# The score scale put into the queries, the head biases loaded a head ahead from ScalarE's queue, and the first read-back products put on GpSimd

## The chip, the cores and the metric

The kernel runs on one core of one Trainium2 chip. The metric is the device time of one execution in microseconds. Three timed runs of the kernel before took 1576.5, 1576.89 and 1585.75 us; the median is 1576.89 us.

## What is computed

One encoder layer on a sequence of 1024 frames of width 1024, in float32. From a layer-normed, modulated input `h` one projection gives queries, keys and values of two attention branches of 8 heads each (head width 64) and two gates. The part of the reference that this change touches:

```python
# A) forgetting attention (FoX)
logits = einsum('bqhd,bkhd->bhqk', qb, k) * scale          # scale = 1/sqrt(64)
logits = logits + cq[:, :, :, None] - cum[:, :, None, :]   # cum = cumsum(log sigmoid(f))
logits = where(k_pos <= q_pos, logits, neg)
out = softmax(logits) @ v
# B) chunked attention, 64-frame chunks, own chunk and 8 to the left
logits = einsum('bcqhd,bckhd->bchqk', qc, kb) * scale
logits = logits + bias                                     # rel_table[h, clipped distance]
out = softmax(where(valid, logits, neg)) @ vb
# after both branches
merged = sigmoid(gate_a) * (o_a @ w_br_fox) + sigmoid(gate_c) * (o_c @ w_br_chunk)
mix = merged @ w_out
x = layer_norm(alpha * x + (1 + g1) * mix)
```

A second sub-layer follows (up-projection, causal depthwise convolution, SiLU gate, down-projection, layer norm).

## The kernel before

Every float32 product is made of three TensorE passes over operands split into a high part and a rest (`mm3`, lines 191 to 194). The layer runs in stages: modulation and the first transposes; attention (from about 100 to 720 us of the profile), in which the projections of later heads are worked off between the scores of earlier ones; the merge of the branches and the output projection; the up-projection; the down-projection.

**Attention.** The heads are worked through in pairs `ip`, in the order 4, 5, 6, 7 (chunked branch), 2, 3, 0, 1 (forgetting branch), and in each pair head by head. One head has four steps `g` of two blocks of 128 queries. The code is written so that, at step `n`, the scores of step `n + 1` stand ahead of the weighted sums of step `n`. `scores` (line 425) makes one block: two matmuls `pss` (L434, L435), then on VectorE one fused operation (L448) that adds the head's bias to the scores, scales, and keeps the row maximum `mx`, then the exponential on ScalarE (L454). `probs` turns the result by TensorE transposes `pst` (L488) and splits it on ScalarE (L491) and VectorE (L492) into `pt`; `weighted` multiplies it with the values (`pso`, L502).

**The bias of a head.** `prep` (line 384) is called for a head some steps before its first scores. It fills `m2`, a copy of the keys with its two halves of partitions exchanged (two DMAs, L392 and L393), and then loads the bias, all on SyncE's DMA queue: `fb`, one row of 1024 sums of the forget gate sent to all 128 partitions (L396), or `cb`, 128x640 numbers of the relative table (L399). There are two bias buffers. The raw scores are not scaled, so the bias has to be divided by the scale: `fb` is stored so (L334), and `cb` is multiplied in place by `scaled()` (line 405) on VectorE (L409), which then fills the two 64x64 corners outside the band with a large negative number (L410, L411). `scaled()` is called where the next step belongs to another head, ahead of the scores of that step.

**GpSimd.** Beside attention GpSimd prepares later weights (`side_work`): products and sums for the modulation, splits and differences, with its own loads and stores of 512 KB. The sums go through two buffers `acc` and are gathered on TensorE (`psada`, L163).

**Softmax sums.** Once per two pairs `inverted` (line 457) turns the sums of a pair, takes reciprocals into `rt` (L463), and stores them to `rd`. `rt` takes a buffer of the tag `fm`, of which there are two; in the forgetting branch the masked diagonal biases `fm` (L441) go through the same two.

**Reading back.** The unnormalised outputs of the heads are stored to `od` (`o32`). `load_o` (line 778) loads two pairs of half a sequence from `od` into `ost` and their reciprocals from `rd` into `ort`, multiplies them on VectorE (L786), and splits the product into `oh` and `ol` (L789, L790). Its first half is called for the pairs 4, 6, 2 and 0, three of them ahead of the last projections.

**The order of the work.** What is written is reordered when the program is built: the build places the instructions of each engine by its own estimate of when their operands are there, and keeps to that order. Each engine then works its own queue strictly in that order: an instruction that waits holds everything behind it on its engine. DMAs are issued by an instruction on the queue of SyncE, ScalarE or GpSimd, and the same holds for them.

## Time and profile before

| what | value |
|---|---|
| timed runs | 1576.5, 1576.89, 1585.75 us |
| profiled execution, its own time | 1572.65 us |
| its span from first to last instruction | 1570.9 us |
| TensorE busy | 1509.7 us, 96% |
| VectorE busy | 1081.9 us, 69% |
| ScalarE busy | 708.2 us, 45% |
| GpSimd busy | 641.5 us, 41% |
| granted TensorE clock, mean | 0.990 |

The time of the profiled execution is the span and 1.75 us around it. In the rows, PE is TensorE and PEld its loads of stationary operands, DVE is VectorE, ACT ScalarE, POOL GpSimd and SP SyncE; a `q` behind the engine marks its queue, as where a DMA is issued. `out<-in` are the program's names, without buffer numbers. A view of waits reads: engine, name and line that waited, after the arrow what ended the wait, then microseconds in total, how many times, and the longest. A view of stretches gives, for each stretch of the span, its length, the busy time of each engine with its instructions, the mean granted clock of TensorE, the busy share of the DMA engines and what they moved.

### The profile page before, as it was taken

The numbers are of one execution on the slowest core, as the hardware profiler recorded it, in microseconds if no ns is written. First come the engines' busy times: TensorE is split into PE (matmuls) and PEld (weight loads), VectorE is DVE, ScalarE is ACT, GpSimd is POOL, SyncE is SP. The second block draws the span as 40 slices with busy tenths as digits, with TensorE's granted clock in tenths as the row PEclk, the third lists the DMA queues.
The fourth block names the chain that finished last, engine by engine and source line by source line (L and its number), as shares of the span: only waits on it lengthen the run. The fifth ranks groups of instructions, "written<-read, shape, count | busy, mean of one in ns | idle before, by whom it ended". The sixth has DMA issues, their size and how long they took to land.

```text
span 1570.9 us, 21838 instructions
## 1 busy us (share of the span) xinstructions
PE 1509.7 (96%) x7663; PEld 1268.5 (81%) x7663; DVE 1081.9 (69%) x2161; ACT 708.2 (45%) x1316; POOL 641.5 (41%) x579
## 2 busy tenths in 40 slices
PE   6999989999999999899998999999999999999996
PEld 3788788889888888788886887888888888788885
DVE  6747566567757676564449488677778876845798
ACT  3545444554445454342102256445454454555451
POOL 0038988888788876100000003545445453000000
PEclk9999999999999999999999999999999999999999
DMA  9156665756666788426999676344333332697552
GB/s 370 40 168 221 216 207 198 233 194 201 220 202 201 253 280 273 172 99 228 307 339 336 242 255 207 104 173 155 133 121 120 129 112 103 223 342 256 196 187 76
DMA packets 130399, 317.81 MB, mean 202 GB/s; under 512 B 12897, under 2 KB 21809, under 8 KB 130289
## 3 DMA queue, kind: packets, MB, share of 16 engines
q1 hardware_dynamic: 94192, 207.79, 39.5%
q0 software_dynamic: 24432, 88.88, 16.6%
q10 hardware_dynamic: 11664, 19.75, 3.4%
q8 instruction: 60, 0.98, 0.3%
q14 instruction: 51, 0.41, 0.1%
HBM read 223.73 MB, written 84.25 MB: 196 GB/s over the span
## 4 chain that ended last, share of the span: by engine, by line
PE 80%; DVE 9%; DMA 7%; issue 2%; ACT 1%; SPq 0%; DVEq 0%; ACTq 0%
PE psu L852 24%; PE pso L502 4%; PE psd L1270 4%; PE psd L1271 4%; PE psd L1269 4%; PE pst L488 3%; PE psg L192 3%; PE psg L193 3%; PE psg L194 3%; PE psq L193 3%; PE psq L194 3%; PE psq L192 3%; DMA cb<-in_rel_t 2%; PE pss L434 2%; PE pss L435 2%; PE psv L295 2%
## 5 line engine op out<-in xcount | busy, mean ns | idle before, releaser
L852 PE MATMUL psu<-hc,wx 128*128 128x512 f32 x792 | 185.7, 389 | 0.1
L852 PEld LDWEIGHTS psu<-hc,wx 128*128 128x128 f32 x792 | 148.6, 188 | 31.4 <-ACT u L1195 0.5
L1118 DVE SCALAR_TENSOR_TENSOR pcv<-u,convp,pcv 128x1024 f32<-128x1024 f32 x88 | 113.2, 1286 | 45.4 <-ACT pcv L1116 44.5
L454 ACT ACTIVATE s<-s,mx 128x640 f32<-128x640 f32 (+7 forms) x128 | 94.5, 738 | 78.6 <-DVE mx L448 77.0
L1259 DVE TENSOR_TENSOR op<-rw,op 128x512 fp32r<-128x512 f32 x146 | 93.3, 688 | 52.9 <-ACT op L1258 52.6
L1258 ACT CAST op<-rw 128x512 fp32r<-128x512 f32 x146 | 85.2, 623 | 84.3 <-PE psd L1271 40.8
L1270 PE MATMUL psd<-op,op 128*128 128x512 f32 x292 | 113.6, 389 | 1.0 <-DVE op L1259 1.0
L1271 PE MATMUL psd<-op,op 128*128 128x512 f32 x292 | 113.6, 389 | 0.0
L491 ACT CAST pt<-pst 128x512 fp32r<-128x512 f32 (+1 forms) x192 | 82.5, 450 | 68.8 <-PE pst L488 67.3
L1269 PE MATMUL psd<-op,op 128*128 128x512 f32 x292 | 113.1, 389 | 0.0
L987 POOL DMA_DIRECT2D xd<-xr x8 | 4.3, 542 | 263.1 <-DVE xr L985 263.1
L192 PE MATMUL psq<-h1h,wh 128*128 128x512 f32 x256 | 104.4, 409 | 1.7 <-DVE h1h L188 1.3
L492 DVE TENSOR_TENSOR pt<-pst,pt 128x512 fp32r<-128x512 f32 (+1 forms) x192 | 96.5, 519 | 13.2 <-ACT pt L491 11.3
L192 PE MATMUL psg<-h1h,wh 128*128 128x512 f32 x256 | 104.6, 409 | 0.0
L194 PE MATMUL psg<-h1h,wl 128*128 128x512 f32 x256 | 100.6, 393 | 1.5 <-DVE wl L112 1.5
L194 PE MATMUL psq<-h1h,wl 128*128 128x512 f32 x256 | 101.2, 395 | 0.9 <-DVE wl L112 0.9
L193 PE MATMUL psq<-h1l,wh 128*128 128x512 f32 x256 | 101.5, 396 | 0.0
L193 PE MATMUL psg<-h1l,wh 128*128 128x512 f32 x256 | 100.7, 393 | 0.0
L502 PE MATMUL pso<-pt,vs 128*128 128x256 f32 x608 | 93.2, 292 | 6.4 <-DVE pt L492 6.2
L550 POOL TENSOR_SCALAR dr<-dr,cond 128x512 f32<-128x512 f32 x56 | 95.7, 1711 | 5.1 <-DMA dr<-in_w_ada 4.1
L502 PEld LDWEIGHTS pso<-pt,vs 128*128 128x128 f32 x608 | 82.9, 194 | 15.2 <-DVE pt L492 8.5
L488 PE MATMUL pst<-ident,s 128*128 128x128 f32 x528 | 83.7, 275 | 8.9 <-DVE pt L492 8.7
(284 smaller groups left out, 4013.7 us busy)
## 6 DMA issues: line engine op xcount, KB each, us to landing
ws<-in_w_up SPq DMA_DIRECT2D x34, 512.0 KB, 3.8
dr<-in_w_ada POOLq DMA_DIRECT2D x32, 512.0 KB, 4.7
dr<-in_w_down POOLq DMA_DIRECT2D x22, 512.0 KB, 5.2
td<-dr POOLq DMA_DIRECT2D x22, 512.0 KB, 5.4
rw<-td SPq DMA_DIRECT2D x44, 256.0 KB, 4.6
yd<-y SPq DMA_DIRECT2D x20, 512.0 KB, 2.8
rw<-yd SPq DMA_DIRECT2D x40, 256.0 KB, 4.6
rw<-sd SPq DMA_DIRECT2D x33, 256.0 KB, 4.6
```

Source lines behind the costliest of these rows:

```text
L192: pe.matmul(ps, wh, xh, start=start, stop=False)
L193: pe.matmul(ps, wh, xl, start=False, stop=False)
L194: pe.matmul(ps, wl, xh, start=False, stop=stop)
L488: pe.transpose(ps[:, b * P : (b + 1) * P], st[:, c0 : c0 + P], ident)
L492: ve.tensor_sub(out=dl, in0=src, in1=dh)
L502: pe.matmul(ps[:, 0:256], vs[:, h % 2, j0 + j, :], pt[j // 4][:, c, j % 4, :], start=j == 0 and c == 0, stop=j == nj - 1 and c == 1)
L550: po.tensor_scalar_mul(x[:, k % 2, :] if k else acc, x[:, k % 2, :], cond[:, k : k + 1])
L852: pe.matmul(ps, w[:, a_, k, :], h[k][b_], start=first, stop=k == 3 and a_ == 1, skip_group_check=on)
L1118: ve.scalar_tensor_tensor(out=ps, in0=u[b][:, 2 - d : S + 2 - d], scalar=cp[:, 2 - d : 3 - d], in1=ps, op0=ALU.mult, op1=ALU.add)
L1269: pe.matmul(ps[t], g[:, 0, ts], d[:, 0], start=start, stop=False, skip_group_check=on)
L1270: pe.matmul(ps[t], g[:, 0, ts], d[:, 1], start=False, stop=False, skip_group_check=on)
L1271: pe.matmul(ps[t], g[:, 1, ts], d[:, 0], start=False, stop=stop, skip_group_check=on)
```

## The change

The scale is put into the queries. `qk_half` gets a factor: for queries ScalarE multiplies where it copied, and VectorE makes the rest with one SCALAR_TENSOR_TENSOR (scale times score, minus the high part) where it had a subtraction; keys stay as they were. The bias then needs no division: `fb` is stored unscaled, `scaled()` with its multiplication (L409) is gone, and the fused operation takes -1 for the scale.

The loading of a bias leaves `prep` for `load_bias(n)`, which is called for the first head before everything, and for each further head at the first step of the head before it. It issues its DMAs on ScalarE's queue. For `cb` there are two, of 64 partitions and 576 columns each, and GpSimd fills the two corners that they leave out. That is 16 issues for the eight chunked heads and 8 for the others.

`rt` of the pairs 2 and 0 takes a buffer of the tag `acc`. In the first half's `load_o` the first three of four rounds issue their DMAs from GpSimd and multiply there.

```diff
-        se.mul(out=fr, in_=ps3[0:n, 0:P], mul=-1.0 / SCALE)
+        se.mul(out=fr, in_=ps3[0:n, 0:P], mul=-1.0)
...
             own, other = slice(i * DH, (i + 1) * DH), slice((1 - i) * DH, (2 - i) * DH)
-            se.copy(out=dst[i][own, sl], in_=ps[own, :])
-            ve.tensor_sub(out=dst[i][other, sl], in0=ps[own, :], in1=dst[i][own, sl])
+            if scale is None:
+                se.copy(out=dst[i][own, sl], in_=ps[own, :])
+                ve.tensor_sub(out=dst[i][other, sl], in0=ps[own, :], in1=dst[i][own, sl])
+            else:
+                se.mul(out=dst[i][own, sl], in_=ps[own, :], mul=scale)
+                ve.scalar_tensor_tensor(out=dst[i][other, sl], in0=ps[own, :], scalar=scale, in1=dst[i][own, sl],
+                                        op0=ALU.mult, op1=ALU.subtract)
...
+    def load_bias(n):
+        if n >= 2 * len(plan):
+            return
+        ip, i = plan[n // 2][0], n % 2
+        br, pr = divmod(ip, 4)
+        h = 2 * pr + i
         if br == 0:
             b = ap.tile([P, S], F32, name=nm("fb"), tag="bias")
-            sy.dma_start(out=b, in_=fd.rearrange("(h t) s -> h (t s)", h=NHEAD)[h].partition_broadcast(P))
+            se.dma_start(out=b, in_=fd.rearrange("(h t) s -> h (t s)", h=NHEAD)[h].partition_broadcast(P))
         else:
             b = ap.tile([P, 640], F32, name=nm("cb"), tag="bias")
-            sy.dma_start(out=b, in_=a["rel_t"][h])
-            unscaled.append(b)
-        return q[i], m1, m2, b, br, h
-    unscaled = []
-    def scaled():
-        while unscaled:
-            b = unscaled.pop(0)
-            ve.tensor_scalar_mul(b, b, 1.0 / SCALE)
-            ve.memset(b[0:DH, 576:640], NEG)
-            ve.memset(b[DH:P, 0:64], NEG)
+            po.memset(b[0:DH, 576:640], NEG)
+            po.memset(b[DH:P, 0:64], NEG)
+            se.dma_start(out=b[0:DH, 0:576], in_=a["rel_t"][h, 0:DH, 0:576])
+            se.dma_start(out=b[DH:P, 64:640], in_=a["rel_t"][h, DH:P, 64:640])
+        biases[ip, i] = b
...
-                    out=st[:, off + s0_ : off + s1_], in0=ps[:, s0_:s1_], in1=b, scale=-SCALE,
+                    out=st[:, off + s0_ : off + s1_], in0=ps[:, s0_:s1_], in1=b, scale=-1.0,
...
-        rt = ap.tile([P, P], F32, name=nm("rt"), tag="fm", bufs=2)[0:n, :]
+        if ip >= 4:
+            rt = ap.tile([P, P], F32, name=nm("rt"), tag="fm", bufs=2)[0:n, :]
+        else:
+            rt = ap.tile([P, H], F32, name=nm("rt"), tag="acc", bufs=2)[0:n, 0:P]
...
+            if g == 0:
+                load_bias(n // 4 + 1)
...
-                    if steps[n][:2] != steps[n + 1][:2]:
-                        scaled()
...
-    def load_o(half, os_, pairs, pool, tag, bufs, rpool, rtag):
-        for i in pairs:
+    def load_o(half, os_, pairs, pool, tag, bufs, rpool, rtag, early=0):
+        for n, i in enumerate(pairs):
+            dma, eng = (po, po) if n < early else (sy, ve)
...
-            ve.tensor_tensor(out=st, in0=st, in1=rt, op=ALU.mult)
+            eng.tensor_tensor(out=st, in0=st, in1=rt, op=ALU.mult)
...
-    reading = load_o(0, o0, (4, 6, 2, 0), ap0, "qs", 4, ap0, "m1")
+    reading = load_o(0, o0, (4, 6, 2, 0), ap0, "qs", 4, ap0, "m1", 3)
```

In the built program the order on TensorE stays as it was but for two short places in attention. The places below are on the engines that lose or gain work. The first is VectorE's queue early in the chunked branch, between the splits `pt` of one block and the next: `cb_1953` is the bias of the fourth head, `pt` the split probabilities, `s` the biased scores and `o` the output of a head. Before:

```order
L448 ISA s_1712,mx_1716<-pss_1713,cb_1574 128x128
L507 TENSOR_TENSOR o_234_1314<-pso_1691,ot_1704 64x256
L409 TENSOR_SCALAR cb_1953<-cb_1953 128x640
L410 MEMSET cb_1953 64x64
L411 MEMSET cb_1953 64x64
L492 TENSOR_TENSOR pt_1707<-pst_1720,pt_1707 128x4x128
L492 TENSOR_TENSOR pt_1708<-pst_1727,pt_1708 128x128
```

Now, at the same place:

```order
L456 ISA s_1712,mx_1716<-pss_1713,cb_1426 128x128
L518 TENSOR_TENSOR o_234_1317<-pso_1694,ot_1707 64x256
L503 TENSOR_TENSOR pt_1710<-pst_1720,pt_1710 128x4x128
L503 TENSOR_TENSOR pt_1711<-pst_1727,pt_1711 128x128
L456 ISA s_1750,mx_1754<-pss_1751,cb_1426 128x256
```

The multiplication and the two fills are no longer between `o` and the split `pt`; the third head's bias is called `cb_1426` now, and the lines are moved by 8 to 11.

The second place is ScalarE's queue shortly before that one; `s_1623` and `s_1626` are the same last scores of the second head, `sg` is a gate. Before:

```order
L491 CAST pt_1577<-pst_1642 128x2x128
L454 ACTIVATE s_1623,sums<-s_1623,mx_1632 128x640
L380 ACTIVATE sg_1684<-psg_1649 128x512
L381 DMA gd<-sg_1684 128x512
L506 COPY ot_1704<-pso_1691 64x256
```

Now:

```order
L502 CAST pt_1580<-pst_1645 128x2x128
L462 ACTIVATE s_1626,sums<-s_1626,mx_1635 128x640
L417 DMA cb_1801<-in_rel_t 64x576
L418 DMA cb_1801<-in_rel_t 64x576
L385 ACTIVATE sg_1687<-psg_1652 128x512
L386 DMA gd<-sg_1687 128x512
L517 COPY ot_1707<-pso_1694 64x256
```

The two issues for the fourth head's bias stand directly behind the exponential of the second head's last scores.

The third place is VectorE's queue near the end of attention, where the second product of the reading back stood. Before:

```order
L441 TENSOR_TENSOR fm_7215<-fb_6958,cmask 128x128
L492 TENSOR_TENSOR pt_7078<-pst_7090,pt_7078 128x4x128
L492 TENSOR_TENSOR pt_7079<-pst_7097,pt_7079 128x3x128
L786 TENSOR_TENSOR ost_7954<-ost_7954,ort_7956 128x1024
L448 ISA s_7137,mx_7143<-pss_7138,fb_6958 128x128
```

Now it stands on GpSimd's queue, behind the last of its side work (`dr` and `td` are tiles of that work):

```order
L593 TENSOR_TENSOR dr_6762<-dr_6762 128x512
L600 DMA td<-dr_6762 128x2x512
L793 DMA ost_7944<-od 128x2x512
L797 DMA ort_7946<-rd 64x2x512 x2
L798 TENSOR_TENSOR ost_7944<-ost_7944,ort_7946 128x1024
L797 DMA ort_7956<-rd 64x2x512 x2
L797 DMA ort_7966<-rd 64x2x512
L793 DMA ost_7954<-od 128x2x512
L797 DMA ort_7966<-rd 64x2x512
L798 TENSOR_TENSOR ost_7954<-ost_7954,ort_7956 128x1024
```

All three early products (`ost_7944`, `ost_7954`, `ost_7964`) and their loads stand there, and the next thing on that queue is a store of the output projection's stage (L999, `xd`).

More of the change, by code (lines that the diff above doesn't have):

```diff
@@ L341, in qk_tiles, with qk_half @@
         return dst
-    def qk_half(dst, w, half):
+    def qk_half(dst, w, half, scale):
         sl = halves(half)
@@ L360, in run @@
                 for i in range(len(which)):
-                    yield from qk_half(dst[i], ws[i], half)
+                    yield from qk_half(dst[i], ws[i], half, None if which[i] else SCALE)
         return Unit([(a["w_qk"][2 * ip + w], [P, KD, P]) for w in which], run, 10.4 * len(which))
@@ L717, in cost_of @@
         return 0.62 * pv_span(ip // 4, g)[1]
+    load_bias(0)
     ensure(0)
-    scaled()
     sts = {(0, i): scores(0, i) for i in range(2)}
@@ L741, in body @@
                         ensure(n + 1)
-                    if steps[n][:2] != steps[n + 1][:2]:
-                        scaled()
                     sts[n + 1, qt] = scores(n + 1, qt)
@@ L776, in body @@
     o_cm, op_ = opened(name="o", bufs=1, side="right")
-    def load_o(half, os_, pairs, pool, tag, bufs, rpool, rtag):
-        for i in pairs:
+    def load_o(half, os_, pairs, pool, tag, bufs, rpool, rtag, early=0):
+        for n, i in enumerate(pairs):
+            dma, eng = (po, po) if n < early else (sy, ve)
             st = pool.tile([P, 2, H], F32, name=nm("ost"), tag=tag, bufs=bufs)
-            sy.dma_start(out=st, in_=od[half, i : i + 2].rearrange("b p s -> p b s"))
+            dma.dma_start(out=st, in_=od[half, i : i + 2].rearrange("b p s -> p b s"))
             rt = rpool.tile([P, 2, H], F32, name=nm("ort"), tag=rtag, bufs=4)
@@ L784, in load_o @@
                 row = rd.rearrange("(p h) s -> h p s", h=2)[h, i : i + 2, halves(half)]
-                sy.dma_start(out=rt[h * DH : (h + 1) * DH], in_=row.partition_broadcast(DH))
-            ve.tensor_tensor(out=st, in0=st, in1=rt, op=ALU.mult)
+                dma.dma_start(out=rt[h * DH : (h + 1) * DH], in_=row.partition_broadcast(DH))
+            eng.tensor_tensor(out=st, in0=st, in1=rt, op=ALU.mult)
             hi = op_.tile([P, 2, H], F32R, name=nm("oh"), tag=f"oh{i}")
```

2 lines of the change are left out of this document (added).

## The prediction

> **What bounds the kernel now.** I read the page's busy shares first, then the waits of TensorE, then the stretches around those waits.
>
> ```profile
> PE 1509.7 (96%) x7663; PEld 1268.5 (81%) x7663; DVE 1081.9 (69%) x2161; ACT 708.2 (45%) x1316; POOL 641.5 (41%) x579
> ```
>
> TensorE is busy for 1509.7 of the span's 1570.9 us. It is the bound, its order hardly changes, and no matmul is added or taken away. So the change can only be worth the time in which TensorE stands still or runs at a lower granted clock, 61 us in all, and of that only what hangs on the instructions that go. Its waits in attention, and VectorE's:
>
> ```profile
> PE pst L488 <- DVE pt L492: 8.7, 5, 3.4
> PE pso L502 <- DVE pt L492: 6.2, 3, 4.6
> PE pss L434 <- DVE mx L448: 2.5, 3, 1.5
> ...
> DVE cb L409 <- DMA cb<-in_rel_t: 14.5, 6, 3.5
> DVE ost L786 <- DMA ost<-od: 9.8, 2, 9.1
> DVE fm L441 <- DMA rd<-rt: 3.0, 2, 2.4
> ```
>
> TensorE waits for `pt`, an ordinary split of 0.7 us. But VectorE itself waited, at the head of its queue, for three loads: the bias to be scaled, the read-back outputs, and the store of the reciprocals that frees an `fm` buffer. What it cannot reach behind them is the `pt` that TensorE wants. The timeline of VectorE (start, duration, idle time before in brackets) at the longest two:
>
> ```profile
> 158.25 0.43 DVE L507 TENSOR_TENSOR o<-pso,ot 64x256 f32<-64x256 f32 x1
> 161.76 1.92 DVE L409 TENSOR_SCALAR cb<-cb 128x640 f32<-128x640 f32 x1 [3.08 <-DMA cb<-in_rel_t]
> ...
> 631.70 1.16 DVE L492 TENSOR_TENSOR pt<-pst,pt 128x512 fp32r<-128x512 f32 x2
> 641.97 1.23 DVE L786 TENSOR_TENSOR ost<-ost,ort 128x1024 f32<-128x1024 f32 x1 [9.11 <-DMA ost<-od]
> ```
>
> How much of that reaches TensorE is the length of a stretch less its busy time. These are the stretches around each stall, and the two that follow the longest:
>
> ```profile
> 108.00:116.00 8.00, 6.51 (x33) 5.03 (x32) 5.64 (x16) 4.53 (x12) 5.28 (x6) 1.00 1.02 337
> 158.00:164.80 6.80, 3.43 (x18) 2.71 (x17) 3.54 (x9) 1.18 (x5) 6.14 (x7) 1.00 0.68 221
> 164.80:168.20 3.40, 3.40 (x11) 2.92 (x12) 1.46 (x5) 1.24 (x4) 3.36 (x5) 0.50 0.63 196
> 197.00:206.00 9.00, 6.71 (x37) 5.62 (x36) 7.38 (x17) 3.32 (x10) 8.93 (x9) 1.00 0.57 189
> 237.00:243.00 6.00, 4.22 (x36) 4.02 (x35) 5.20 (x15) 2.26 (x8) 5.97 (x7) 1.00 0.32 94
> 548.00:552.00 4.00, 3.18 (x19) 2.44 (x18) 3.05 (x9) 0.76 (x4) 3.27 (x5) 1.00 0.77 266
> 632.00:644.78 12.78, 8.19 (x42) 6.74 (x40) 3.55 (x9) 2.13 (x5) 5.49 (x6) 0.92 0.96 355
> 644.78:649.48 4.70, 4.70 (x20) 4.50 (x21) 2.62 (x5) 2.17 (x5) 0.00 (x0) 0.50 0.41 131
> ```
>
> **The change part by part.** *The bias no longer scaled on VectorE.* Four stalls stand at an L409: 8.00 - 6.51 = 1.49, 6.80 - 3.43 = 3.37, 9.00 - 6.71 = 2.29 and 6.00 - 4.22 = 1.78 us, together 8.93. The other four L409 cost TensorE nothing. After the longest the granted clock is 0.50 for 3.40 us, in which full speed would have needed about half: 1.70. The splits behind L409 have their operands by then, so that whole stall goes. VectorE also loses eight multiplications, of 1.46 us on average in these rows:
>
> ```profile
> L409 DVE TENSOR_SCALAR cb<-cb 128x640 f32<-128x640 f32 x8 | 11.6, 1455 | 14.5 <-DMA cb<-in_rel_t 14.5
> L353 DVE TENSOR_TENSOR qm<-psq,qm 64x512 fp32r<-64x512 f32 x60 | 41.2, 687 | 9.8 <-ACT qm L352 8.3
> L921 DVE SCALAR_TENSOR_TENSOR sgl<-sgl,psb 128x512 f32<-128x512 f32 x16 | 10.7, 675 | 5.9 <-PE psb L194 3.1 <-DMA sgl<-gd 2.8
> ```
>
> The new operation on the queries is a SCALAR_TENSOR_TENSOR of 512 columns from PSUM: 675 ns where there is one, against 687 for the subtraction it replaces. Nothing, to either side; the same for ScalarE's multiplication in place of its copy, one pass over 512 columns either way.
>
> *The load a head ahead.* Will VectorE now wait for the bias at its first use instead? The issue stands behind the exponential of the head before last. The tightest place is the third head, whose issue comes behind the exponential of the first head's last scores:
>
> ```profile
> 128.08 0.40 ACT L454 ACTIVATE s<-s,mx 128x128 f32<-128x128 f32 x1 [1.62 <-DVE mx L448]
> ...
> 157.95 0.26 DVE L448 CUSTOM_DVE_ANT_0 s<-pss,cb 128x128 f32<-128x128 f32 x1
> ...
> DMA to landing us min/median/max: 4.9/6.8/7.7
> ```
>
> The last row is the landing of today's `cb` loads. From 128.6 to 157.95 there are 29 us for 7.7 at most. The corners have the same lead: GpSimd may fill them once VectorE has read the old bias, and nothing reads them until then. GpSimd is held for that read at most, and its own deadline is far: its sum `acc` ends here at 467.8 and TensorE fetches it at 511.4.
>
> ```profile
> 466.52 1.29 POOL L553 TENSOR_TENSOR acc<-acc,dr 128x512 f32<-128x512 f32 x1
> ...
> 511.43 0.95 PE L163 MATMUL psada<-ones,acc 128*128 128x1 f32 x8
> ```
>
> So 44 us cover the fills; were that cover gone, TensorE would wait at `psada`. Only the first head has no head before it. Its issue moves behind ScalarE's copy of the queries, which the next rows show ending at 103.05, where SyncE issued it at 104.32:
>
> ```profile
> 102.47 0.58 ACT L352 CAST qm<-psq 64x512 fp32r<-64x512 f32 x1
> 104.32 0.71 SPq L399 DMA_DIRECT2D cb<-in_rel_t  x1
> ```
>
> A landing by 111.5 (7.7 after the second issue), without the scaling and the filling that VectorE now does behind its landing (1.46 us the scaling alone, by the row above), is before TensorE ran dry at 113.45 - 1.49 = 111.96. I count the 1.49 as gained. The Trainium skill speaks against the two halves, in "DMA: Bandwidth & Descriptors", section "Rules for kernel authors": transfers to disjoint partition halves serialise, and one 128-partition transfer is better. By it the halves would land at 103.1 + 2 x 4.9 = 112.9 at best, and the sum below would be 1.5 smaller; no run here shows a bias in halves, and for all other heads the lead covers twice 7.7.
>
> *The issues on ScalarE.* 24 issues. ScalarE's own cost today, and SyncE's for the same loads:
>
> ```profile
> L381 ACTq DMA_DIRECT2D gd<-sg x32: 326/326/385, 142.8 to 730.9; - x32
> ...
> L396 SPq DMA_DIRECT2D fb<-fd x8: 326/490/1268, 337.3 to 624.0; - x8
> ...
> L399 SPq DMA_DIRECT2D cb<-in_rel_t x8: 328/595/2464, 104.3 to 303.1; - x8
> ```
>
> (minimum, median and maximum in ns.) At 0.326 that is 7.8 us of ScalarE, which is idle for 55% of the span. Behind each issue stand the copies `pt` and `ot`. If all were hidden it costs 0, if none 7.8. TensorE waited for ScalarE's `pt` in steps of 0.3 us (the row follows), so ScalarE is seldom late; I take 1.0.
>
> ```profile
>   ACT pt L491: 2.7, 10
> ```
>
> SyncE's queue loses these issues, and the loads of weights behind them no longer wait for a bias buffer; I give that nothing.
>
> *`rt` in an `acc` buffer.* The next rows are from the timelines of VectorE, ScalarE and SyncE's queue; the first belongs here, the others to the products.
>
> ```profile
> 548.85 0.29 DVE L441 TENSOR_TENSOR fm<-fb,cmask 128x128 f32<-128x128 f32 x1 [2.37 <-DMA rd<-rt]
> ...
> 721.09 1.05 ACT L789 CAST oh<-ost 128x1024 fp32r<-128x1024 f32 x1 [1.38 <-DVE o L507]
> 667.15 0.38 SPq L781 DMA_DIRECT2D ost<-od  x1
> ```
>
> VectorE's 2.37 us for the store at 548.85 goes, and with it 4.00 - 3.18 = 0.82. The buffer was last read by TensorE 30 us before, by the rows of `acc` above, so no wait comes in its place.
>
> *The products on GpSimd.* The stall of 12.78 - 8.19 = 4.59 goes, and half of the 4.70 us at clock 0.50 behind it, 2.35. GpSimd's queue has nothing else until the next stage, and ScalarE takes the products only at 721, against a GpSimd finish of some 680 (its third load issues where SyncE's did, at 667). What is late next on VectorE is `pt` itself, with its operands there. A price: GpSimd's product reads two tiles, 1.33 us per 512 columns, so 2.65 each.
>
> ```profile
> L547 POOL TENSOR_TENSOR dr<-dr,dr 128x512 fp32r<-128x512 f32 x32 | 41.7, 1327 | 0.4
> L112 DVE TENSOR_TENSOR wl<-ws,wh x38: 1201/1226/3799, 25.0 to 702.6; 128x1024 fp32r<-128x1024 f32 x38
> ```
>
> VectorE's split of weights, L112, takes 1.2 us mostly and up to 3.8 while GpSimd works. So three products may hold VectorE for 0 to 8 us (3 x 2.65). TensorE followed L112 in few of its cases; I take 0.4. The Trainium skill has the reason, in "SBUF — State Buffer", section "Who interferes with whom": a VectorE instruction with two SBUF inputs contends with a GpSimd instruction that reads SBUF. Taken at its word for all three, the sum would be 7.6 smaller; the spread of L112 agrees with it, not with its happening each time.
>
> *Sum.* 8.93 + 1.70 + 0.82 + 4.59 + 2.35 = 18.4, less 1.0 and 0.4: 17.0. Against the profiled execution's 1572.65 us that is 1555.7. This execution ran 4.2 us below the median of the timed runs, so for the median of 1576.89 I predict 1559.9, say 1560.
>
> **The rivals.**
>
> *Part is given back* (1568). With the stalls gone VectorE and ScalarE lose the time in which they caught up, and smaller waits that were hidden come out. For it: stalls without any load before them, as at L112, exist already. Against it: VectorE is at 69%, and sheds 15 us. If half returns the gain is 8 to 9.
>
> *The DMA stage takes it* (1576). From 720 us the merge runs with DMAs near their limit:
>
> ```profile
> 720.00:800.00 80.00, 80.00 (x355) 66.23 (x354) 33.82 (x43) 13.21 (x17) 0.00 (x0) 1.00 0.93 296
> 840.00:870.00 30.00, 24.99 (x97) 19.26 (x96) 24.11 (x67) 8.08 (x13) 1.61 (x3) 0.89 0.97 356
> ```
>
> If transfers, not TensorE, set the pace there, arriving 17 us earlier only lengthens the 5 us of stall at 840 to 870. Against it: TensorE is busy for 80.00 of 80.00 us, and the loads start as buffers come free, so they move with it.
>
> *The corners or the issue come late* (1571). Then VectorE waits at the first use, and the bias terms, 8.9 + 1.7, are not won. Against it stand the leads of 29 and 44 us.
>
> *ScalarE's queue is held, and the kernel is slower* (1589). An issue that takes as long as the longest of `fb`, 1.27 us, stops ScalarE for that time with `pt` behind it. 24 x 1.27 = 30.5, less the 18.0 that the other terms leave: 12 slower. It decides from 18.0 / 24 = 0.75 us lost by TensorE per issue; the longest `cb` issue shows that 2.46 can occur. Against it: ScalarE's own issues never passed 0.385 us, and its idle share.
>
> **How the numbers follow.** My forecast, 1555 to 1565 with 1560 likeliest, has 60%; part given back 22%, the DMA stage 8%, late corners or issue 5%, a held ScalarE 5%. The range goes from 1553 (the 18.4 in full, and 5 us of the remaining waits for VectorE with them) to 1572; it leaves out the DMA stage, the held queue and a rest, under 2 in 10. One per cent, about what a measurement of this kernel can tell from no change, is 15.8 us: faster below 1561.1. Nearly four fifths of the forecast lie there, hence 0.48 faster, 0.47 within one per cent, 0.05 slower.
>
> **What would show it.** Right: no VectorE wait for `cb` or `ost`; TensorE's waits for `pt` down from 14.9 to about 3; no clock of 0.50 near 165 and 645; ScalarE's issues of bias near 0.33 us; products on GpSimd done some 40 us before ScalarE takes them; from about 630 us the same stages 17 us earlier. Wrong: VectorE's L456 waiting for a bias DMA or for GpSimd; a longer L112 between 640 and 680 with TensorE behind it; more than 5 us of TensorE idle at the output projection; ScalarE issues over 0.75 us.

## The result and the profile after

The changed kernel takes 1556.28 us (median of 4 runs, 1553.31 to 1558.97) against 1577.02 us of the kernel before (4 runs, 1576.5 to 1585.75). The ratio is 0.9877, 95% interval 0.9842 to 0.9911: faster by 1.2%. Its profiled execution has a span of 1551.5 us and took 1553.31 us, 19.3 us less than that of before. The first line of its page:

```profile
PE 1503.7 (97%) x7663; PEld 1266.4 (82%) x7663; DVE 1071.6 (69%) x2134; ACT 709.2 (46%) x1316; POOL 657.5 (42%) x607
```

TensorE is busy 6.0 us less (1509.7 before), although it runs the same matmuls. Most of that is time at half clock that is gone: before 720 us the kernel before has granted clock 0.50 for 3.41, 3.41 and 6.83 us, the changed kernel once, for 3.41 us. The other 13.4 us of the span are time in which it stood still. The waits in attention (engine and line that waited, what for, us in total, times, longest):

```profile
PE pso L513 <- DVE pt L503: 3.8, 2, 2.2
...
DVE fm L449 <- DMA rd<-rt: 3.4, 1, 3.4
...
DVE s L456 <- POOL cb L415: 2.0, 1, 2.0
...
PE pst L499 <- DVE pt L503: 1.5, 2, 0.9
```

TensorE's waits for the split `pt` fell from 14.9 to 5.3 us. VectorE's 14.5 us for the bias and 9.8 us for the read-back outputs are gone; in their place stand 2.0 us for a corner that GpSimd filled late, and 3.4 us for the reciprocal row that still lies in an `fm` buffer. The stretches that answer to those of before (us of the stretch, then busy us and instructions of PE, PEld, DVE, ACT, POOL, granted clock, DMA share, GB/s):

```profile
105.00:113.00 8.00, 8.00 (x42) 6.43 (x40) 5.23 (x14) 5.99 (x13) 3.03 (x3) 1.00 1.02 299
154.00:158.00 4.00, 4.00 (x26) 3.48 (x25) 1.95 (x8) 1.50 (x5) 3.08 (x4) 1.00 1.03 318
190.00:194.00 4.00, 4.00 (x23) 3.42 (x22) 2.20 (x7) 1.54 (x7) 2.50 (x3) 1.00 0.70 262
225.00:230.00 5.00, 5.00 (x45) 5.00 (x44) 2.21 (x8) 2.72 (x7) 4.97 (x6) 1.00 0.16 28
328.00:332.00 4.00, 3.10 (x17) 2.50 (x17) 2.55 (x8) 1.11 (x5) 3.77 (x5) 1.00 0.02 4
458.00:464.00 6.00, 4.40 (x25) 3.38 (x24) 6.00 (x11) 2.04 (x5) 5.98 (x7) 1.00 0.75 245
592.00:604.00 12.00, 9.79 (x47) 8.32 (x46) 11.65 (x19) 4.46 (x9) 9.85 (x11) 0.86 0.81 269
620.00:640.00 20.00, 20.00 (x111) 17.16 (x110) 12.11 (x35) 8.92 (x20) 14.30 (x15) 1.00 0.82 284
```

The first four hold the places of the four bias stalls, the last that of the read-back: TensorE is busy throughout, at granted clock 1.00. The three between them are new stalls: 0.90, 1.60 and 2.21 us, the last with half clock behind it.

Where the time went can be followed matmul by matmul, since both programs run 7663 of them in nearly the same order. The table gives, for stretches named by the time in the kernel before, by how many us the same matmul moved against that kernel within the stretch (negative is a gain). The last column is the sum. It is worked out from the starts of the matmuls in the traces, also for the experiments that follow. Each row compares two single executions, and these can lie some us from the median of their kernel: the profiled one of the kernel before is 4.4 us below its median, that of the bias part alone 7 below, that of the load ahead with late scaling 5 above.

| us of before | to 95 | 95-275 | 275-520 | 520-625 | 625-665 | 665-985 | 985-1545 | sum |
|---|---|---|---|---|---|---|---|---|
| changed kernel | -1.0 | -14.1 | +1.8 | +1.3 | -7.0 | -0.2 | -0.3 | -19.4 |
| bias part alone | +0.4 | -15.0 | +1.3 | -0.4 | -6.8 | -0.5 | +0.3 | -20.6 |
| read-back alone | -0.3 | -1.5 | +0.3 | +0.7 | -7.0 | +2.5 | 0.0 | -5.2 |
| scale alone | -1.1 | -10.7 | +4.5 | +5.7 | -4.9 | -0.2 | +0.1 | -6.8 |
| ahead, scaled early | -1.4 | -1.0 | +9.6 | +1.9 | -6.2 | -1.7 | -0.1 | +1.2 |
| ahead, scaled late | +0.3 | -12.0 | -0.9 | +9.3 | -3.0 | +2.8 | +8.4 | +5.0 |
| bias part, SyncE's queue | +0.3 | -11.4 | -3.4 | +9.0 | -0.9 | -1.7 | 0.0 | -8.2 |
| changed, SyncE's queue | +0.4 | -14.0 | +2.7 | -1.0 | -7.0 | -0.4 | +0.2 | -19.2 |
| changed, GpSimd copies | +0.1 | -12.2 | -2.5 | -1.2 | -6.9 | +2.1 | -0.4 | -21.0 |
| changed, corners once | -1.0 | -12.3 | +3.7 | -0.4 | -6.8 | +0.5 | +0.2 | -16.2 |

The gain comes in two places, 95 to 275 and 625 to 665 us, and some 3 us are given back between them. The microsecond before 95 us is not the change's: it arises at 52 us, where the profile of before has half clock and that of after has not, behind a stall that both have (the last section comes back to it).

### The profile page after: what moved, and what is told of

The parts are those of the page before. It is cut to its first block, busy times and chain, and to the rows that moved or that the text cites. A ratio compares the mean times of both kernels' runs of the same rounds, so it can differ in the third digit from the quotient of the medians.

```text
span 1551.5 us, 21888 instructions
## 1 busy us (share of the span) xinstructions
PE 1503.7 (97%) x7663; PEld 1266.4 (82%) x7663; DVE 1071.6 (69%) x2134; ACT 709.2 (46%) x1316; POOL 657.5 (42%) x607
## 3 DMA queue, kind: packets, MB, share of 16 engines
q0 software_dynamic: 25344, 92.02, 17.5%
## 5 line engine op out<-in xcount | busy, mean ns | idle before, releaser
L502 ACT CAST pt<-pst 128x512 fp32r<-128x512 f32 (+2 forms) x192 | 82.7, 451 | 71.1 <-PE pst L499 67.2
L503 DVE TENSOR_TENSOR pt<-pst,pt 128x512 fp32r<-128x512 f32 (+2 forms) x192 | 96.6, 519 | 13.8 <-ACT pt L502 12.2
L561 POOL TENSOR_SCALAR dr<-dr,cond 128x512 f32<-128x512 f32 x56 | 91.2, 1630 | 12.4 <-DMA dr<-in_w_ada 11.4
L999 POOL DMA_DIRECT2D xd<-xr x8 | 4.4, 544 | 209.7 <-DVE xr L997 209.7
```

The lines of the kernel that those rows point to most:

```text
L503: ve.tensor_sub(out=dl, in0=src, in1=dh)
```

## The experiments

**One part alone.** The bias part is the change without the products on GpSimd and without `rt` in an `acc` buffer:

```diff
-    reading = load_o(0, o0, (4, 6, 2, 0), ap0, "qs", 4, ap0, "m1", 3)
+    reading = load_o(0, o0, (4, 6, 2, 0), ap0, "qs", 4, ap0, "m1")
...
-        if ip >= 4:
-            rt = ap.tile([P, P], F32, name=nm("rt"), tag="fm", bufs=2)[0:n, :]
-        else:
-            rt = ap.tile([P, H], F32, name=nm("rt"), tag="acc", bufs=2)[0:n, 0:P]
+        rt = ap.tile([P, P], F32, name=nm("rt"), tag="fm", bufs=2)[0:n, :]
```

> The kernel before with the scale in the queries and the biases loaded a head ahead on ScalarE's queue with the corners on GpSimd; the read-back products and the reciprocal rows stay as they were. My theory (a load at the head of VectorE's queue holds the splits that TensorE wants): the four stalls at the bias go, the stall of 4.6 us at 640 to 645 and the half clock behind it stay. Gain about 10.6 us, so about 1566. Rival (the stalls of VectorE beside GpSimd take part of it back): 4 to 7 us, 1570 to 1573.

Measured: 1559.43 us, ratio 0.9876 (0.9835 to 0.9916): not to be told from the whole change, and a larger gain than I expected. The read-back part alone is the kernel before with `load_o` as changed:

```diff
-            sy.dma_start(out=st, in_=od[half, i : i + 2].rearrange("b p s -> p b s"))
+            dma.dma_start(out=st, in_=od[half, i : i + 2].rearrange("b p s -> p b s"))
...
-            ve.tensor_tensor(out=st, in0=st, in1=rt, op=ALU.mult)
+            eng.tensor_tensor(out=st, in0=st, in1=rt, op=ALU.mult)
```

> The kernel before with only the first three read-back products and their loads put on GpSimd. My theory: the stall of 4.59 us and half of the 4.70 us at clock 0.50 behind it go, 6.9 us, and nothing before 640 us changes, so about 1570. Rival (the products hold VectorE's two-operand work): 8 us of VectorE, up to 7.6 us lost, so about 1577.

Measured: 1567.42 us, ratio 0.9931 (0.9903 to 0.9959). By the medians the parts bring 17.5 and 9.6 us alone and 20.7 together. With intervals of 4 to 6 us to either side the times alone do not show that the parts fail to add up. The table shows it for one stall: each part removes the one at 640 us (-6.8 and -7.0), and it can be removed only once. How the bias part does it is on SyncE's queue. The rows are from the timelines of SyncE (start, us, the issue), first in the kernel before:

```profile
623.29 0.59 SPq L393 DMA_DIRECT2D m<-qm  x1
623.97 0.85 SPq L396 DMA_DIRECT2D fb<-fd  x1
629.42 0.33 SPq L104 DMA_DIRECT2D ws<-in_w_g  x1
629.80 0.43 SPq L781 DMA_DIRECT2D ost<-od  x1
```

Then with the bias part alone:

```profile
609.71 0.59 SPq L398 DMA_DIRECT2D m<-qm  x1
610.35 0.63 SPq L789 DMA_DIRECT2D ost<-od  x1
611.03 1.72 SPq L793 DMA_DIRECT2D ort<-rd  x1
615.51 0.33 SPq L104 DMA_DIRECT2D ws<-in_w_g  x1
```

Before, the load `ost` stood behind the weights `ws`, which waited 4.6 us (629.42 less 624.82) for a free buffer. Without `fb` in that queue the scheduler put `ost` ahead of `ws`: it is issued 0.64 us after the copy of the keys and not 6.5 us after it.

**The queue by itself.** To see whether that is the cause, the bias part alone with its loads on SyncE's queue:

```diff
-            se.dma_start(out=b, in_=fd.rearrange("(h t) s -> h (t s)", h=NHEAD)[h].partition_broadcast(P))
+            sy.dma_start(out=b, in_=fd.rearrange("(h t) s -> h (t s)", h=NHEAD)[h].partition_broadcast(P))
...
-            se.dma_start(out=b[0:DH, 0:576], in_=a["rel_t"][h, 0:DH, 0:576])
-            se.dma_start(out=b[DH:P, 64:640], in_=a["rel_t"][h, DH:P, 64:640])
+            sy.dma_start(out=b[0:DH, 0:576], in_=a["rel_t"][h, 0:DH, 0:576])
+            sy.dma_start(out=b[DH:P, 64:640], in_=a["rel_t"][h, DH:P, 64:640])
```

> The run with only the bias part, which gave 1559.4, with the biases' loads issued on SyncE's queue at the same places of the program. My theory (the loads that stand behind a bias in SyncE's queue wait for the bias buffer): the second read-back load is issued some 5 to 10 us later again, the stall near 640 us comes back with its half clock, 5 to 7 us, 1565 to 1567. Rival (the queue doesn't matter, the stalls of the bias and their following cost were all): 1559.

Measured: 1562.3 us (1551.3 to 1567.7), too wide a spread to tell 1559 from 1565. Its trace is clear. Two rows of its SyncE timeline, and the stretches of two stalls:

```profile
623.45 0.34 SPq L104 DMA_DIRECT2D ws<-in_w_g  x1
623.84 0.52 SPq L789 DMA_DIRECT2D ost<-od  x1
```

```profile
533.00:540.00 7.00, 2.08 (x11) 1.69 (x10) 5.60 (x9) 0.91 (x3) 5.41 (x7) 0.75 0.69 269
632.00:640.00 8.00, 3.65 (x17) 2.94 (x17) 4.26 (x9) 2.33 (x5) 7.54 (x8) 0.93 0.86 296
```

`ost` is behind `ws` again, and TensorE stands still for 8.00 - 3.65 = 4.35 us. The order is not all that sets this stall. In the run with the scale alone (below) the order is the old one, but `ws` waited only 2.0 us, `ost` was issued at 626.40 and TensorE stood still for 1.76 us, without half clock. In the run with the late multiplication (below) `ost` stood ahead of `ws`, but took 14.0 us to land, and TensorE stood still for 1.76 us as well. The stall at 533 (4.92 us) is the one that `rt` in an `acc` buffer was to prevent: VectorE waited 1.56 us there for the store of `rt`, and its mask sum then took 3.25 us. Next, the whole change with the same three lines on SyncE's queue:

> The changed kernel with the bias loads issued on SyncE's queue at the same places; the read-back products and their loads stay on GpSimd. My theory (SyncE's queue cost time only through the read-back load that stood behind a weight load in it): the stall near 640 does not come back, 1555 to 1559. Rival A (ScalarE's issues of 0.33 to 1.1 us cost TensorE): 3 to 8 us faster than the changed kernel, 1548 to 1553. Rival B (SyncE's queue holds other loads too): 1561 to 1565.

Measured: 1552.85 us (1551.16 to 1553.76), ratio 0.9829 (0.9799 to 0.9859). With the read-back off that queue the stall does not come back. The median is 3.4 us below that of the changed kernel, as rival A has it, but the profiled executions are level (spans 1551.8 and 1551.5) and TensorE waited for ScalarE's `pt` as before. The changed kernel was not timed again beside this run and the other late ones; beside them the median of the kernel before was 1580.3 us, and 1577.0 beside the changed kernel, so differences of some 3 us from 1556.28 say little. Whether ScalarE's issues cost TensorE anything stays open.

**Multiplication or wait?** The scale alone takes the multiplication away and leaves the load and VectorE's fills where they were:

```diff
         while unscaled:
             b = unscaled.pop(0)
-            ve.tensor_scalar_mul(b, b, 1.0 / SCALE)
             ve.memset(b[0:DH, 576:640], NEG)
```

> The kernel before with only the scale put into the queries: VectorE's multiplication of the bias is gone, but the load stays where it was on SyncE's queue and VectorE still fills the corners behind it. My theory (the wait for the load counts): VectorE still waits some 14 us for the bias, each of the four stalls shrinks by its own multiplication alone (0.74 to 1.9 us), so some 3 us of the 8.9 remain: gain 5 to 7 us, 1570 to 1572. Rival (VectorE's work of 8 x 1.46 us is what counts): the whole 10.6, 1566.

Measured: 1569.23 us, ratio 0.9957 (0.9928 to 0.9985). The wait for the bias, and the stretches of the two stalls that remain of the four:

```profile
DVE cb L414 <- DMA cb<-in_rel_t: 16.5, 6, 4.3
```

```profile
108.00:112.00 4.00, 2.76 (x14) 1.90 (x13) 1.99 (x8) 2.26 (x4) 2.31 (x2) 1.00 1.05 326
156.00:161.00 5.00, 3.48 (x19) 2.75 (x18) 1.66 (x8) 1.14 (x4) 4.96 (x6) 1.00 0.87 284
```

1.24 + 1.52 = 2.76 us are left of 8.93, although VectorE waits as long as ever. The other half is the load a head ahead, with the multiplication and the fills kept on VectorE:

```diff
-            sy.dma_start(out=b, in_=a["rel_t"][h])
-            unscaled.append(b)
+            se.dma_start(out=b, in_=a["rel_t"][h])
+            unscaled[n] = b
...
+            if g == 0:
+                load_bias(n // 4 + 1)
```

> The kernel before with only the bias loaded a head ahead on ScalarE's queue (whole loads of 128 partitions); the multiplication and the fills stay on VectorE at their place. My theory (the wait for the load counts): no wait of VectorE for the bias, all four stalls and the half clock at 165 us gone, 9 to 10.6 us, 1566 to 1568. Rival (VectorE's work counts): nothing, 1577.

Measured: 1574.94 us, ratio 0.9994: no gain. But the run did not make the case that it was meant to make. Its wait for the bias, the multiplication and the issue that it waited for:

```profile
DVE cb L420 <- DMA cb<-in_rel_t: 24.4, 5, 10.8
...
161.57 0.52 DVE L420 TENSOR_SCALAR cb<-cb 128x640 f32<-128x640 f32 x1 [7.60 <-DMA cb<-in_rel_t]
...
153.21 0.35 ACTq L410 DMA_DIRECT2D cb<-in_rel_t  x1
```

The scheduler moved the multiplication forward with the load, and at 153.97 VectorE stood in front of a load issued 0.8 us earlier; TensorE lost 4.94 us there and 4.99 at 310. In the next run the factor is made from a fresh maximum, so that the multiplication cannot move forward:

```diff
+                ve.tensor_scalar(out=k, in0=last[-1], scalar1=0.0, scalar2=1.0 / SCALE, op0=ALU.mult, op1=ALU.add)
+                ve.tensor_scalar_mul(b, b, k)
```

> Again the kernel before with only the bias loaded a head ahead on ScalarE's queue and multiplied on VectorE, but the factor is a number that VectorE makes from a maximum of the newest scores, so that the multiplication can't be put early in VectorE's queue, where in the run before it waited up to 10.8 us for its load. My theory (the wait for a load at the head of the queue counts, not the multiplication's 1.46 us): VectorE's waits for the bias go to about 0, and with them the stalls; with the loads also off SyncE's queue about 1562 to 1568. Rival (VectorE's work counts): no gain, 1574 to 1577.

Measured: 1572.57 us (1568.0 to 1578.2), ratio 0.9982 (0.9958 to 1.0006): outside what my theory gave, and outside what the rival gave. The wait for the bias is 1.1 us in all, and between 95 and 275 us the run gains 12.0, as the theory says. It loses 9.3 between 520 and 625, where two stalls of 2.54 and 2.57 us came, each with 3.41 us of half clock behind it. So the early stage is settled: either half, the multiplication gone or the wait gone, brings 10.7 to 12.0 of the 14 to 15 us there. What an early gain is worth at the end is another question, and it hangs on the stalls after 275 us.

**The stalls after 275 us.** VectorE at two of the new stalls of the changed kernel:

```profile
458.44 3.75 DVE L449 TENSOR_TENSOR fm<-fb,cmask 128x128 f32<-128x128 f32 x1
...
592.38 3.21 DVE L449 TENSOR_TENSOR fm<-fb,cmask 128x128 f32<-128x128 f32 x2
```

The mask sum of 128x128 takes 3.75 us. Of the 64 in the changed kernel's trace, the 37 that ran beside no two-operand operation of GpSimd took 0.28 us on average (0.22 to 0.29, nine of them beside GpSimd's multiplication by a number), the 27 beside one took 1.48 (0.27 to 4.16). In the kernel before it is 0.29 (two of nine beside the multiplication took 0.56 and 0.57) and 1.23. The test takes these operations off GpSimd:

```diff
-            po.tensor_tensor(out=acc, in0=acc, in1=x[:, k % 2, :], op=ALU.add)
+            po.tensor_scalar_mul(acc, x[:, k % 2, :], cond[:, k : k + 1])
```

> The changed kernel with every two-operand operation of GpSimd beside attention replaced by a multiplication by a number of the same size, so the sums and the low parts of the later weights are left out and the output is another. In the trace of the changed kernel VectorE's mask sum of 128x128 takes 0.28 us beside no work of GpSimd and beside its one-operand work, but 0.28 to 4.16 us beside a two-operand operation. My theory (that contention made the new stalls of 1.6 us at 461 and 2.2 us at 597): all mask sums near 0.28 us, the splits of weights at 1.2 us, both stalls and the half clock behind the second gone, 4 to 8 us, 1548 to 1552. Rival (those stalls come from the order of the work): 1555 to 1557.

Measured: 1573.1 us, 17 us slower than the changed kernel. All mask sums took less than 0.73 us, and yet the run lost, as these two rows show (all mask sums: least, median and longest ns; VectorE's timeline):

```profile
L449 DVE TENSOR_TENSOR fm<-fb,cmask x64: 216/284/722, 363.5 to 681.3; 128x128 f32<-128x128 f32 x64
...
712.22 2.19 DVE L798 TENSOR_TENSOR ost<-ost,ort 128x1024 f32<-128x1024 f32 x1 [13.95 <-issue]
```

The multiplication by a number is slower on GpSimd than the sum (1.6 against 1.3 us), so its side work ended at 679 and not at 647 us, its products came late, and VectorE's own fourth product stood 14 us in the queue: an 11.3 us stall. A corner came 5.6 us late as well. The run tests GpSimd's lateness as much as contention. With copies instead, GpSimd is early:

```diff
-            po.tensor_tensor(out=acc, in0=acc, in1=x[:, k % 2, :], op=ALU.add)
+            po.tensor_copy(out=acc, in_=x[:, k % 2, :])
```

> Once more the changed kernel without two-operand operations of GpSimd beside attention, now with copies in their place, which take about 0.65 us instead of 1.6, so that GpSimd's queue is early instead of some 40 us late; sums and differences of the later weights are left out. My theory (contention makes the new stalls near 461 and 597): mask sums near 0.3 us, both stalls and the half clock gone, no late corner, no stall at a product: 1548 to 1552. Rival (order of the work makes them): 1555 to 1557.

Measured: 1551.29 us (1549.27 to 1552.02), ratio 0.9820 (0.9795 to 0.9845), 5.0 us under the changed kernel's median, which is from another round of runs. The two stretches again:

```profile
458.00:464.00 6.00, 6.00 (x34) 4.94 (x32) 4.54 (x19) 2.76 (x8) 5.05 (x7) 1.00 0.76 241
592.00:604.00 12.00, 11.49 (x61) 9.61 (x60) 8.97 (x22) 6.11 (x13) 3.52 (x3) 1.00 0.48 132
```

Of 1.60 and 2.21 us there remain 0.00 and 0.51, and the half clock is gone. Between 275 and 625 us this run gains 3.7 us where the changed kernel gives back 3.1. So GpSimd's two-operand work, against copies in its place, costs this kernel some 5 to 7 us. That price is not contention alone: the copies are also shorter (some 0.65 us against 1.3), so GpSimd is earlier and overlaps less. At 458 to 464 it is busy for 5.05 of 6.00 us, so being idle does not explain that place. The mask sums are not all short here either: beside copies 14 of them took 0.59 us on average and up to 1.41.

**Product or load?** The read-back part moves both to GpSimd. First the loads stay there and the products go back to VectorE:

```diff
-            dma, eng = (po, po) if n < early else (sy, ve)
+            dma, eng = (po, ve) if n < early else (sy, ve)
```

> The changed kernel with the three early read-back loads still on GpSimd's queue but the products back on VectorE at their places. My theory (the late load was the stall, not the product's 1.23 us): the loads are in time, 1555 to 1558, no stall over 1 us at a product. Rival (VectorE can't bear the product there): the stall of 4.6 us and the half clock are back, 1560 to 1563.

Measured: 1623.52 us, 67 us slower than the changed kernel. Then the other way round:

```diff
-            dma, eng = (po, po) if n < early else (sy, ve)
+            dma, eng = (sy, po) if n < early else (sy, ve)
```

> The changed kernel with the early read-back loads back on SyncE's queue and only the three products on GpSimd. In the run with the products on VectorE and the loads on GpSimd's queue the loads stood behind the last of GpSimd's own work, and VectorE waited 67.6 us. My theory now (what helped is that the products left VectorE; the loads' queue matters only for a product that has to wait there): same as the changed kernel, 1554 to 1558, GpSimd finds its operands landed. Rival (the loads on SyncE's queue hold the weights): a stall behind a split of weights after 610 us, 1559 to 1563.

Measured: 1591.33 us, 35 us slower. Both expectations were far off. The first run, GpSimd's end of side work and VectorE's first product:

```profile
640.30 0.73 POOL L600 DMA_DIRECT2D td<-dr  x1 [0.45 <-POOL dr L593]
641.03 0.73 POOL L793 DMA_DIRECT2D ost<-od  x1
...
649.25 1.23 DVE L798 TENSOR_TENSOR ost<-ost,ort 128x1024 f32<-128x1024 f32 x1 [67.59 <-DMA ort<-rd]
```

On GpSimd's queue the loads are not early at all: they stand behind its last side work, at 641 us, while VectorE's product had its place at 582. The second run, rows of SyncE, GpSimd and ScalarE:

```profile
564.70 73.76 SPq L797 DMA_DIRECT2D ort<-rd  x3
...
635.50 2.35 POOL L798 TENSOR_TENSOR ost<-ost,ort 128x1024 f32<-128x1024 f32 x1
...
642.71 0.33 ACTq L280 DMA_DIRECT2D od<-o  x1
```

The third load of reciprocals needs a buffer that the first product frees. That product is behind GpSimd's side work, so SyncE's queue stood from 565 to 638 us with keys and weights behind it; ScalarE stopped at its own store, which by the trace was released when that load landed, and TensorE stood for 37.7 us. The change works because loads and products moved together, to a queue on which nobody waits for them.

**Two more waits removed.** Two standing bias tiles whose corners are filled once, and `rt` always in an `acc` buffer:

```diff
-            b = ap.tile([P, 640], F32, name=nm("cb"), tag="bias")
-            po.memset(b[0:DH, 576:640], NEG)
-            po.memset(b[DH:P, 0:64], NEG)
+            b = bias_bufs[n % 2][:, 0:640]
+            if n < 2:
+                po.memset(b[0:DH, 576:640], NEG)
+                po.memset(b[DH:P, 0:64], NEG)
```

> The changed kernel with two standing bias tiles, whose corners GpSimd fills once at the start (the loads leave them alone), and with the reciprocal rows of all pairs in an acc buffer. In the changed kernel one fill stood behind GpSimd's work and held VectorE 2.0 us (TensorE 0.9 us), and the one reciprocal row left in an fm buffer held VectorE 3.4 us (TensorE some 0.6 us). My theory (those two waits are real losses): neither wait in the trace, 1 to 2 us less, 1554 to 1555, which the timed runs can hardly tell from 1556. Rival (other waits take their place): 1556 to 1558.

Measured: 1555.07 us (1553.53 to 1556.83), ratio 0.9846 (0.9820 to 0.9872): not to be told from the changed kernel. Both waits are gone from its trace. In its profiled execution another stall took their place, of 2.84 us with 6.83 us of half clock, behind a split of weights beside GpSimd's two-operand operations:

```profile
454.71 6.19 DVE L112 TENSOR_TENSOR wl<-ws,wh 128x1024 fp32r<-128x1024 f32 x1 [4.07 <-ACT wh L111]
```

## Why the prediction was right, point by point

The time is 1556.28 us, 3.7 below the 1560 that I forecast and inside the range, and the gain is over 1%, to which I gave 0.48. The steps behind it were not all right; some errors cancelled. In the table the stage of the bias brought 3.5 us more than its term, of which 1.6 are luck (below), while 3.1 came back later, against 1.4 that I had taken off.

- *What bounds.* Right: the gain is time in which TensorE stood still (13.4 us) and busy time (6.0 us), most of it at half clock. My 61 us, the span less the busy time, were the standstill alone; time at half clock counts as busy and comes on top.
- *The bias.* The places were right, and all four stalls are gone. The term was too small: 8.93 + 1.70 = 10.63, against 14.1 us between 95 and 275. Followed matmul by matmul, the four stalls brought 10.0 us and the half clock 1.5. Of the rest, 0.7 us came between 115 and 157 us, about the second and the third L409 (125.88 and 130.41), so "the other four L409 cost TensorE nothing" was not quite so; 0.7 came between 213 and 220. The largest piece, 1.6 us, is a stall at 210 us that is none of the bias's. There TensorE waited for a split of weights. The split before, GpSimd beside it, and the same split in the changed kernel:

```profile
207.55 3.80 DVE L112 TENSOR_TENSOR wl<-ws,wh 128x1024 fp32r<-128x1024 f32 x1 [2.12 <-ACT wh L111]
207.71 2.55 POOL L547 TENSOR_TENSOR dr<-dr,dr 128x512 fp32r<-128x512 f32 x2
...
196.37 1.53 DVE L112 TENSOR_TENSOR wl<-ws,wh 128x1024 fp32r<-128x1024 f32 x1 [2.12 <-ACT wh L111]
```

VectorE stood idle 2.12 us ahead of it in both, so it was not behind. The split was long before, beside two of GpSimd's two-operand products, and short now, beside a multiplication by a number and a copy. In the two runs that keep this stall, the read-back alone and the load ahead with early scaling, it took 3.76 and 3.94 us, beside the same products; in the bias part alone 1.23. What GpSimd does at that moment was not in my prediction, and that it fell well is luck.

That multiplication and wait make the bias stalls together, and that either half removed takes most of them, I had not said either.

- *The load a head ahead.* Right for seven of eight heads. For the last chunked head the fill stood behind GpSimd's multiplications of the side work; VectorE waited 2.0 us and TensorE 0.90. My cover of 44 us was that of GpSimd's deadline, and did not ask when GpSimd's own queue gets to the fill. The rival of late corners is thus real, at a tenth of its price.
- *The halves.* The first head's two loads, issued at 101.48 and 102.06, took 3.2 and 5.2 us to landing (the whole load of before 7.6), so both had landed at 107.3, ahead of the first use at 109.13.

```profile
L418 ACTq DMA_DIRECT2D cb<-in_rel_t x1: 834/834/834, 102.1 to 102.1; - x1
...
DMA to landing us min/median/max: 5.2/5.2/5.2
```

The price that I had worked out beside it from the Trainium skill ("DMA: Bandwidth & Descriptors", section "Rules for kernel authors": halves serialise, one whole transfer is better) did not arise: by it the second half would have landed at 112.9. My pricing was wrong, each half taken as a whole load of 4.9 us; the rule is not refuted, since the second half landed 2.6 us after the first, though issued 0.58 after it. Over the eight heads the second half's median is 7.4 us and the first's 5.1, but here no one waits for it.

- *The issues on ScalarE.* The size was wrong, the effect was not seen. The rows of the changed kernel's sixteen half loads and eight others (ns: least, median, longest):

```profile
L417 ACTq DMA_DIRECT2D cb<-in_rel_t x8: 472/478/977, 101.5 to 287.7; - x8
L418 ACTq DMA_DIRECT2D cb<-in_rel_t x8: 499/817/1112, 102.1 to 288.2; - x8
L412 ACTq DMA_DIRECT2D fb<-fd x8: 326/326/327, 321.7 to 611.3; - x8
```

By the medians that is 13 us, not 7.8. Some passed 0.75 us, where the rival of the held queue was to decide, but no loss of TensorE shows: its waits for ScalarE's `pt` are the same (2.7 us before, 2.6 now, ten each).

- *SyncE's queue.* "I give that nothing" was wrong. In the bias part alone it is worth the whole stall at 640 us, 6.8 us; the changed kernel does not gain it twice, because the read-back term of 4.59 + 2.35 = 6.94 is the same stall (7.0 measured). The sum counted that stall once and so came out right; what it said each part is worth was wrong.
- *`rt`.* VectorE's wait at that place is gone, but the gain of 0.82 cannot be seen in the sum: the stretch from 520 to 625 us lost 1.3, for another stall at 597. In the run of the bias part on SyncE's queue the old buffer had its part in a stall of 4.92 us: 1.56 us of VectorE's wait, and the 3.25 us that the mask sum behind it took.
- *The products on GpSimd.* The first and the last of the three on GpSimd, and ScalarE's first use:

```profile
655.14 2.40 POOL L798 TENSOR_TENSOR ost<-ost,ort 128x1024 f32<-128x1024 f32 x1 [6.18 <-DMA ort<-rd]
...
673.55 2.40 POOL L798 TENSOR_TENSOR ost<-ost,ort 128x1024 f32<-128x1024 f32 x1 [3.48 <-DMA ost<-od]
...
702.31 2.95 ACT L801 CAST oh<-ost 128x1024 fp32r<-128x1024 f32 x3 [1.57 <-issue]
```

They take 2.40 us each, not 2.65, and are done at 676 us: 26 us of cover and not 40. From 665 us on the table shows no loss.
- *What was taken off* (1.0 + 0.4) was too little in the wrong place: about 3 us came back between 275 and 625 us. It is the rival "part is given back" at a third of its size. Its cause was in my text, but only for the three products: VectorE's two-operand operations beside GpSimd's. The rule of the Trainium skill ("SBUF — State Buffer", section "Who interferes with whom") that I quoted there holds for all of GpSimd's side work. The run with copies gives some 5 us for that work, contention and GpSimd's lateness together. The price differs with what GpSimd does: beside its multiplications by a number per partition the mask sum kept its 0.28 us in the changed kernel's trace (nine cases) and took up to 0.57 in the kernel before and 0.72 in the run made of such multiplications, against 1.48 on average and up to 4.16 beside two operands.
- *The DMA stage* did not take the gain: from 665 us to the end the shift changed by 0.5 us, to the better.

## What to carry to other kernels

A stall can need two causes at once, so that removing either ends most of it, and a part that removes one may earn the gain that was booked for another: work out each part alone, and ask whether two terms count the same stall. When a step moves to another engine's queue, its loads, the buffers that it frees and whoever stands behind those loads must move with it; half a move cost 35 to 67 us here. On VectorE a row's mean hides what GpSimd's work beside it costs: 0.28 us alone and up to 4.16 us beside it, for the same instruction. A stall that goes away near an edit need not be the edit's: look at what the instruction waited for, and at what ran beside it, in both traces.

## What the runs showed of the hardware

A stall of TensorE costs more than its length once it is long enough. In the traces of all kernels here, every stall in attention over 3 us, nine of thirteen from 2.05 to 2.84 us and two of five from 1.75 to 1.81 us have 3.41 us or a multiple at granted clock 0.50 at them or within 1.5 us behind; of those of 1.2 to 1.7 us in attention none has. The bound is not sharp: of the 14 executions, 7 had the half clock after the same stall of 1.34 us at 51 us, 7 had not.

The granted clock does not tell all of the pace. In the profiled run with the late multiplication TensorE never stood still in the up-projection, and yet made 432 matmuls in 100 us at granted clock 1.00, where the changed kernel made 443:

```profile
1100.00:1200.00 100.00, 100.00 (x432) 80.49 (x431) 69.89 (x80) 47.73 (x66) 49.08 (x36) 1.00 0.40 137
```

```profile
1100.00:1200.00 100.00, 100.00 (x443) 82.78 (x442) 79.30 (x86) 49.82 (x69) 49.59 (x37) 1.00 0.40 141
```

The first row is from that run, the second from the changed kernel. That is the +8.4 in its row of the table; the edit touches nothing in that stage, and why the pace was lower, no run shows.
